# Branch C's triangular solve: forward by rows instead of columns, its blocks loaded by four transfers, and two short steps before it written otherwise

## The chip, the cores and the metric

The kernel runs on one core of a Trainium2 chip. The metric is device time in microseconds (us) for one call. TensorE (PE) does the matrix products, VectorE (DVE) and ScalarE (ACT) the elementwise work, GpSimd (POOL) some elementwise work and transfers, SyncE (SP) issues most of the transfers.

## The reference

One inference step of a decoder layer for a prompt group (1024 tokens) and a sample group (8 sequences of 8 new tokens). Four parallel token mixers, A to D, read one input projection of x. The change lies in branch C, a state recurrence over tokens with 4 heads of 64:

```
kk = kk / max(sqrt(sum(kk * kk)), 1e-12)
k_eff = k * (1.0 + (a - 1.0) * ka_s)
def step(S, inp):                       # -kk and kk * a are a_t and b_t
    sa = einsum('nhij,nhj->nhi', S, a_t)
    S = S * w_t[:, :, None, :] + sa[..., None] * b_t[:, :, None, :] + v_t[..., None] * k_t[:, :, None, :]
    return S, einsum('nhij,nhj->nhi', S, r_t)
y = (y - m) * rsqrt(var + RW_GN_EPS) * gn_g + gn_b
```

The other branches, the gates, the memory attention and the MLP follow; they are not changed.

## The kernel before

Branch C is done in chunks of 256 prompt tokens (numbers 0 to 3) and one chunk, number 4, for the 64 sample tokens, in the order 0, 4, 1, 2, 3. `branch_c` (L763 on) calls for each chunk `c_pre` (decays, k, r, v and the normalised kk), `c_blocks` (the strictly triangular products L of 128 x 128 per head and block), `c_solve` (the inverse of a unit triangular matrix in diagonal blocks of 32 x 32), `c_uw` (what the inverse is used for), `c_chain` or `c_sample` (the state itself) and `c_norm`. The next chunk's `c_pre`, `c_blocks` and `c_solve` stand in the text ahead of or beside the present chunk's chain.

`c_solve` writes the 32 x 32 diagonal blocks of L to DRAM (`Ld`, L1003), reads them back with one transfer that puts the same 32 blocks on four groups of 32 partitions (`Li`, L1004), and lets each partition carry eight rows of the inverse (`Ti`, which starts as the identity, `teye`, L1008). VectorE sets the diagonal of `Li` to one (L1009) and then makes one column t of `Ti` after the other: a product over all s up to t into `tpr` (L1015), and a sum over s (L1016), 31 columns, 62 instructions, for the sample as for the prompt. `Ti` then goes through DRAM (`Td`, L1018) into the block diagonal `TT` (L1021), from which `c_uw` starts (product u, L1036). `Li` and `Ti` have one buffer each.

`rsqrt` (L922) takes exp(-0.5 ln s) on ScalarE and betters it by one Newton step of five VectorE instructions (L927 to L931). It serves `c_pre` (kk) and `c_norm` at full width, and branch D at a few columns. In `c_pre`, L891 and L892 make k (1 + (a - 1) ka).

Between these steps `fill` puts units of other work into the text: the input projections of D, A and B (products mm, L118 and L130, whose weights come through `split_w`: transfer `wraw`, ScalarE's rounding `whi` L101, VectorE's rest `wlo` L107). Each engine's order is fixed when the program is built, by a planner that takes instructions by their place in the text and by durations of its own; every engine then runs its list in order, and a wait at its head holds all that is behind it. SP's list holds `wraw`, the raw rows of C (`raw<-hC`), `Ld`, `Li`, `teye`, `Td` and `TT` together.

Of the kernel before, what the change touches and what calls it, by code (L numbers as in the profile page):

```python
# [8 lines left out]
F32 = mybir.dt.float32  # L9
F32R = mybir.dt.float32r  # L10
I32 = mybir.dt.int32
AF = mybir.ActivationFunctionType
ALU = mybir.AluOpType
AX = mybir.AxisListType
# [8 lines left out]
C_BG, C_CONV, C_MU, C_W0, C_A0, C_KK, C_KA, C_RK, C_GNG, C_GNB, C_SB = 0, 32, 38, 45, 47, 49, 51, 53, 55, 57, 59  # L23
# [9 lines left out]
def sv(a, x):  # L33
    return a.rearrange("p (s x) -> p s x", x=x)
# [16 lines left out]
class Kern:  # L51
# [721 lines left out]
    def branch_c(self, cc):  # L773
        nc, I, O = self.nc, self.I, self.O
        vec = self.vec
        self.cc = cc
        cm = self.cm = cc.tile([128, 648], F32, name="cmask")
        self.lw = cc.tile([128, 256], F32, name="lw")
        self.smask = cc.tile([128, 320], F32, name="smask")
        self.omu = cc.tile([128, 7], F32, name="omu")  # L780
        for t, x in ((cm, "cmask"), (self.lw, "lora"), (self.smask, "smask")):
            nc.sync.dma_start(t, I[x])
        nc.vector.tensor_scalar(self.omu, vec[:, C_MU:C_MU + 7], -1.0, 1.0, op0=ALU.mult, op1=ALU.add)
        self.bones = cm[:, 0:128]

        self.S = [cc.tile([128, 2, 2, 64], F32, name=f"S{i}") for i in range(2)]
        for t in self.S:
            nc.vector.memset(t, 0.0)
        order = (0, 4, 1, 2, 3)
        TT = self.TT = cc.tile([128, 8, 128], F32, name="TT")  # L790
        nc.gpsimd.memset(TT, 0.0)
        d = self.c_pre(0)
        self.c_blocks(d)
        self.c_solve(d)
        nxt = self.c_pre(order[1])
        self.fill("first")
        for i, c in enumerate(order):
            if nxt:
                self.c_blocks(nxt)
            self.c_uw(d)  # L800
            if nxt:
                self.c_solve(nxt)
            if c < 4:
                self.c_chain(d)
            else:
                self.c_sample(d)
            after = self.c_pre(order[i + 2]) if i < 3 else None
            self.c_norm(d)
            d, nxt = nxt, after
        for hh in range(2):  # L810
            nc.gpsimd.dma_start(O["p_wkv"][HR[hh]], self.S[0][HR[hh], :, hh, :])

    def c_pre(self, c):

        nc, vec, cc = self.nc, self.vec, self.cc
        smp = c == 4
        n, x, o, w = (64, 8, 1025, 72) if smp else (256, 64, 256 * c, 257)
        ns = n // x
        V = lambda q, pr: vec[:, q + pr:q + pr + 1]
# [4 lines left out]
        def shifted(m, k, name, tag="t"):  # L824

            raw, xs = self.ct("raw"), self.cf(name, n, tag)
            nc.sync.dma_start(raw[:, :k, :w], self.hC[:, m:m + k, o:o + w])
            for i in range(k):
                mu, om = vec[:, C_MU + m + i:C_MU + m + i + 1], self.omu[:, m + i:m + i + 1]
                if smp:  # L830
                    cur, prev, out = sv(raw[:, i, 0:72], 9)[:, :, 1:9], sv(raw[:, i, 0:72], 9)[:, :, 0:8], sv(xs[:, i], 8)
                else:
                    cur, prev, out = raw[:, i, 1:n + 1], raw[:, i, 0:n], xs[:, i]
                nc.scalar.mul(out, prev, mu)
                nc.vector.scalar_tensor_tensor(out, cur, om, out, op0=ALU.mult, op1=ALU.add)
            return xs
# [6 lines left out]
        sg, a = self.cf("sg", n), self.cf("aa", n)  # L843
# [8 lines left out]
        k = shifted(2, 2, "xk")  # L852
# [35 lines left out]
        nc.vector.tensor_mul(bh, kk, a)  # L888
        nc.vector.tensor_mul(bh, bh, Pi)
        for pr in range(2):  # L890
            nc.vector.tensor_scalar(a[:, pr], a[:, pr], 1.0, V(C_KA, pr), op0=ALU.subtract, op1=ALU.mult)  # L891
        nc.vector.scalar_tensor_tensor(k, a, 1.0, k, op0=ALU.add, op1=ALU.mult)  # L892
        nc.vector.tensor_mul(kh, k, Pi)
        r = shifted(0, 2, "xr")
        nc.vector.tensor_mul(by(rt), by(r), Pp[:, :, 1:x + 1])
# [4 lines left out]
        for i in range(2):  # L900
            mu, om = vec[:, C_MU + 4 + i:C_MU + 5 + i], self.omu[:, 4 + i:5 + i]
            if smp:
                cur, prev, out = sv(raw[:, i, 0:72], 9)[:, :, 1:9], sv(raw[:, i, 0:72], 9)[:, :, 0:8], sv(v[:, i], 8)
            else:
                cur, prev, out = raw[:, i, 1:n + 1], raw[:, i, 0:n], v[:, i]
# [16 lines left out]
    def rsqrt(self, s, r, out):  # L922

        nc = self.nc
        nc.scalar.activation(r, s, AF.Ln)
        nc.scalar.activation(r, r, AF.Exp, scale=-0.5)
        nc.vector.tensor_mul(s, s, r)  # L927
        nc.vector.tensor_mul(out, out, r)
        nc.vector.tensor_mul(s, s, r)
        nc.vector.tensor_scalar(s, s, -0.5, 1.5, op0=ALU.mult, op1=ALU.add)  # L930
        nc.vector.tensor_mul(out, out, s)  # L931

    def c_blocks(self, d):

# [59 lines left out]
    def c_solve(self, d):  # L994

        nc, cc, c = self.nc, self.cc, d["c"]
        L = d["L"]
        Ld = self.dr.tile([4, 8, 32, 32], F32, name="Ld", tag=f"Ld{c}")
        Li = cc.tile([128, 32, 32], F32, name="Li", tag="Li")
        Ti = cc.tile([128, 8, 32], F32, name="Ti", tag="Ti")  # L1000
        tp = cc.tile([128, 8, 32], F32, name="tpr", tag="tpr")
        for q in range(4):
            nc.sync.dma_start(Ld[q].rearrange("(b h) s t -> s b h t", h=2), L[32 * q:32 * q + 32, :, :, 32 * q:32 * q + 32])  # L1003
        nc.sync.dma_start(Li.rearrange("p s t -> p (s t)"), Ld.rearrange("q i s t -> (q i) (s t)")[None].to_broadcast([4, 32, 1024]))  # L1004
        if c < 4:

            nc.gpsimd.tensor_mul(L, L, self.cm[:, None, None, 384:512].to_broadcast([128, 4, 2, 128]))
        nc.sync.dma_start(Ti, self.I["teye"])  # L1008
        nc.vector.memset(Li.rearrange("p a b -> p (a b)")[:, 0::33], 1.0)  # L1009
        tf = tp.rearrange("p a s -> p (a s)")  # L1010
        for t in range(1, 32):
            h = t // 4 + 1
            tv = tf[:, :h * (t + 1)].rearrange("p (a s) -> p a s", s=t + 1)

            nc.vector.tensor_mul(tv, Ti[:, 0:h, 0:t + 1], Li[:, 0:t + 1, t:t + 1].rearrange("p s o -> p o s").to_broadcast([128, h, t + 1]))  # L1015
            nc.vector.tensor_reduce(Ti[:, 0:h, t:t + 1], tv, axis=AX.X, op=ALU.add)  # L1016
        Td = self.dr.tile([4, 8, 8, 4, 32], F32, name="Td", tag=f"Td{c}")
        nc.sync.dma_start(Td.rearrange("q i l e t -> e (q i) l t"), Ti)  # L1018
        TT = self.TT
        for q in range(4):  # L1020
            nc.sync.dma_start(TT[32 * q:32 * q + 32, :, 32 * q:32 * q + 32], Td[q].rearrange("i l e t -> (l e) i t"))  # L1021
# [1353 lines left out]
```

## Time and profile before

| What | us |
|---|---|
| median of 3 runs | 2223.06 |
| lowest, highest run | 2218.23, 2223.72 |
| the profiled execution's own time | 2223.23 |
| its span | 2221.5 |
| PE busy in the span | 2140.5 (96%) |
| DVE busy | 1338.9 (60%) |
| ACT busy | 944.9 (43%) |
| POOL busy | 421.1 (19%) |

Busy is the time in which an engine had an instruction at work. A wait is the idle time of an engine ahead of an instruction, put down to what ended last before it. PEclk is the share of TensorE's full clock (2.4 GHz) that was granted; 0.50 is the lower level, 1.2 GHz. Branch C's chunks lie between 96 and 450 us of the span.

### The profile page before, as it was taken

The numbers are of one execution on the slowest core, as the hardware profiler recorded it, in microseconds if no ns is written. First come the engines' busy times: TensorE is split into PE (matmuls) and PEld (weight loads), VectorE is DVE, ScalarE is ACT, GpSimd is POOL, SyncE is SP. The second block draws the span as 40 slices with busy tenths as digits, with TensorE's granted clock in tenths as the row PEclk, the third lists the DMA queues.
The fourth block names the chain that finished last, engine by engine and source line by source line (L and its number), as shares of the span: only waits on it lengthen the run. The fifth ranks groups of instructions, "written<-read, shape, count | busy, mean of one in ns | idle before, by whom it ended". The sixth has DMA issues, their size and how long they took to land.

```text
span 2221.5 us, 36111 instructions
## 1 busy us (share of the span) xinstructions
PE 2140.5 (96%) x13674; PEld 1912.7 (86%) x13674; DVE 1338.9 (60%) x2682; ACT 944.9 (43%) x1838; POOL 421.1 (19%) x478
## 2 busy tenths in 40 slices
PE   8988999999999999999999999999999999999998
PEld 8977787888989988998899877779999999788886
DVE  3265778745666665343325583469877766665477
ACT  4343343234555556444323262326444444544341
POOL 0110111112310310013221230000654542100000
PEclk9999999999999999999999999999999999999999
DMA  6322333135543434555415145743686667976552
GB/s 196 98 75 59 100 106 93 41 121 178 152 135 116 151 103 159 172 169 164 128 48 194 57 159 188 251 157 124 239 278 234 237 243 252 322 250 203 166 199 90
DMA packets 184838, 356.11 MB, mean 160 GB/s; under 512 B 36104, under 2 KB 92568, under 8 KB 184664
## 3 DMA queue, kind: packets, MB, share of 16 engines
q1 hardware_dynamic: 174216, 318.24, 43.6%
q0 software_dynamic: 10448, 35.57, 4.7%
q8 instruction: 107, 1.75, 0.3%
q14 instruction: 67, 0.55, 0.1%
HBM read 250.01 MB, written 103.73 MB: 159 GB/s over the span
## 4 chain that ended last, share of the span: by engine, by line
PE 72%; DMA 10%; DVE 10%; ACT 3%; issue 3%; POOL 1%; SPq 1%; DVEq 0%; ACTq 0%; POOLq 0%
PE mm L118 20%; PE m L118 14%; PE dn L2037 13%; PE mm L130 8%; PE sc L130 3%; PE pp L118 3%; PE ds L2042 1%; DVE wlo L107 1%; DVE tpr L1015 1%; ACT whi L101 1%; DMA add<-gate 1%; PE gr L967 1%; DMA wraw<-in_w_gate 1%; DMA Li<-Ld 1%; DMA vp<-in_vpages,pt 1%
## 5 line engine op out<-in xcount | busy, mean ns | idle before, releaser
L118 PE MATMUL mm<-ah,whi 128*128 128x384 f32 (+1 forms) x1176 | 394.6, 336 | 10.3 <-ACT ah L279 5.1
L118 PE MATMUL mm<-al,whi 128*128 128x384 f32 (+1 forms) x1176 | 391.3, 333 | 1.4 <-DVE al L280 1.4
L118 PE MATMUL mm<-ah,wlo 128*128 128x384 f32 (+1 forms) x1176 | 390.7, 332 | 0.6 <-DVE wlo L107 0.6
L2037 PE MATMUL dn<-dop 128*128 128x512 f32 x1344 | 317.1, 391 | 1.9 <-ACT dop L1705 1.9
L2037 PEld LDWEIGHTS dn<-dop 128*128 128x128 f32 x1344 | 252.2, 188 | 56.7 <-ACT dop L1705 2.3
L107 DVE TENSOR_TENSOR wlo<-wraw,whi 128x1024 fp32r<-128x1024 f32 (+2 forms) x145 | 159.1, 1104 | 168.4 <-ACT whi L101 167.7
L118 PEld LDWEIGHTS mm<-ah,whi 128*128 128x128 f32 x1176 | 223.8, 190 | 19.9 <-ACT ah L279 5.4
L101 ACT CAST whi<-wraw 128x1024 fp32r<-128x1024 f32 (+1 forms) x130 | 132.9, 1028 | 227.6 <-PE mm L118 100.4
L118 PEld LDWEIGHTS mm<-al,whi 128*128 128x128 f32 x1176 | 223.2, 190 | 7.1 <-issue 3.3
L118 PEld LDWEIGHTS mm<-ah,wlo 128*128 128x128 f32 x1176 | 223.5, 190 | 4.2 <-issue 1.9
L1706 DVE TENSOR_TENSOR dop<-wraw,dop 128x512 fp32r<-128x512 f32 x224 | 149.1, 696 | 109.2 <-ACT dop L1705 109.0
L118 PE MATMUL m<-xht,wo 128*128 128x272 f32 x1024 | 199.3, 290 | 2.8 <-DVE u L1914 2.6
L1705 ACT CAST dop<-wraw 128x512 fp32r<-128x512 f32 x224 | 133.0, 620 | 153.9 <-PE dn L2037 85.8
L130 PE MATMUL mm<-wlo,ah 128*128 128x512 f32 (+1 forms) x488 | 169.2, 350 | 4.5 <-DVE wlo L107 4.4
L130 PE MATMUL mm<-whi,ah 128*128 128x512 f32 (+1 forms) x488 | 170.2, 351 | 0.6 <-ACT stA L302 0.5
L118 PEld LDWEIGHTS m<-xht,wo 128*128 128x128 f32 x1024 | 162.6, 188 | 3.7 <-ACT u L1734 2.8
L130 PE MATMUL mm<-whi,al 128*128 128x512 f32 (+1 forms) x448 | 156.2, 349 | 0.0
L118 PE MATMUL m<-xh,wo 128*128 128x272 f32 x768 | 150.8, 290 | 0.0
L118 PE MATMUL m<-xlt,wo 128*128 128x272 f32 x512 | 147.7, 289 | 1.4 <-DVE xlt L2184 1.4
L118 PEld LDWEIGHTS m<-xh,wo 128*128 128x128 f32 x768 | 122.4, 188 | 0.1
L118 PE MATMUL m<-xl,wo 128*128 128x272 f32 x384 | 110.7, 289 | 0.0
L130 PEld LDWEIGHTS mm<-wlo,ah 128*128 128x128 f32 x488 | 93.4, 192 | 18.6 <-DVE wlo L107 5.6
(514 smaller groups left out, 4211.2 us busy)
## 6 DMA issues: line engine op xcount, KB each, us to landing
wraw<-hs SPq DMA_DIRECT2D x112, 256.0 KB
wraw<-in_w_up SPq DMA_DIRECT2D x36, 512.0 KB
wraw<-in_w_gate SPq DMA_DIRECT2D x32, 512.0 KB
dw<-in_w_down SPq DMA_DIRECT2D x32, 512.0 KB
hs<-sh SPq DMA_DIRECT2D x64, 256.0 KB
wt<-dw SPq DMA_DIRECT2D x32, 512.0 KB
wraw<-wt SPq DMA_DIRECT2D x64, 256.0 KB
wraw<-in_w_down SPq DMA_DIRECT2D x48, 256.0 KB
```

The lines of the kernel that those rows point to most:

```text
L101: nc.scalar.copy(hi[:, c], raw[:, c])
L107: nc.vector.tensor_sub(lo[:, c], raw[:, c], hi[:, c].bitcast(F32))
L118: nc.tensor.matmul(ps[:, :n], a, b, start=first and i == 0, stop=last and i == len(steps) - 1, skip_group_check=not first)
L130: nc.tensor.matmul(ps[:, :n], a, b, start=i == 0, stop=i == len(steps) - 1)
L967: nc.tensor.matmul(g[hh][:nb, j, :nb], p[HR[hh], pr, cs], q[HR[hh], pr, cs], start=True, stop=True)
L1015: nc.vector.tensor_mul(tv, Ti[:, 0:h, 0:t + 1], Li[:, 0:t + 1, t:t + 1].rearrange("p s o -> p o s").to_broadcast([128, h, t + 1]))
L1705: nc.scalar.copy(o[:, 0], src)
L1706: nc.vector.tensor_sub(o[:, 1], src, o[:, 0].bitcast(F32))
L2037: nc.tensor.matmul(ps[j], hs[:, a, c], w[:, b], start=first and k == 0, stop=last and k == 2, skip_group_check=n >= 16 and steps[n][0] in ...
L2042: nc.tensor.matmul(sp, rows[p][:, smp[i]].rearrange("p a n -> p (a n)"), ops[n][1][:, b], start=i != 2 and p == 0 and b == 0, stop=p == 15 ...
```

## The change

- `c_solve` works by rows s: column s of `Ti` times row s of the blocks, to the right of the diagonal, into `tpr`, and then an addition of that to the rest of `Ti`: 31 rows, 62 instructions for a prompt chunk, over fewer elements. The diagonal is no longer used and no longer set.
- For the sample, whose blocks within each 32 x 32 are four of 8 x 8, one row of all four is done at once by a strided view: 7 rows, 14 instructions. The tiles get a row more for that view.
- `Li` is loaded by four transfers of 32 partitions, and `teye` stands ahead of `Ld` in the text.
- `rsqrt`'s Newton step has four VectorE instructions instead of five.
- (1 - ka) + a ka is made by two ScalarE instructions, and VectorE's product with k has no addition in it.

```diff
+        self.oka = cc.tile([128, 2], F32, name="oka")
+        nc.vector.tensor_scalar(self.oka, vec[:, C_KA:C_KA + 2], -1.0, 1.0, op0=ALU.mult, op1=ALU.add)
...
         for pr in range(2):
-            nc.vector.tensor_scalar(a[:, pr], a[:, pr], 1.0, V(C_KA, pr), op0=ALU.subtract, op1=ALU.mult)
-        nc.vector.scalar_tensor_tensor(k, a, 1.0, k, op0=ALU.add, op1=ALU.mult)
+            nc.scalar.activation(a[:, pr], a[:, pr], AF.Identity, scale=V(C_KA, pr), bias=self.oka[:, pr:pr + 1])
+        nc.vector.tensor_mul(k, a, k)
...
-        nc.vector.tensor_mul(s, s, r)
+        nc.vector.scalar_tensor_tensor(s, s, -0.5, r, op0=ALU.mult, op1=ALU.mult)
         nc.vector.tensor_mul(out, out, r)
         nc.vector.tensor_mul(s, s, r)
-        nc.vector.tensor_scalar(s, s, -0.5, 1.5, op0=ALU.mult, op1=ALU.add)
-        nc.vector.tensor_mul(out, out, s)
+        nc.vector.scalar_tensor_tensor(out, s, 1.5, out, op0=ALU.add, op1=ALU.mult)
...
-        Li = cc.tile([128, 32, 32], F32, name="Li", tag="Li")
-        Ti = cc.tile([128, 8, 32], F32, name="Ti", tag="Ti")
-        tp = cc.tile([128, 8, 32], F32, name="tpr", tag="tpr")
+        Li = cc.tile([128, 33, 32], F32, name="Li", tag="Li")
+        Ti = cc.tile([128, 9, 32], F32, name="Ti", tag="Ti")
+        tp = cc.tile([128, 80], F32, name="tpr", tag="tpr")
+        nc.sync.dma_start(Ti[:, 0:8], self.I["teye"])
...
-        nc.sync.dma_start(Li.rearrange("p s t -> p (s t)"), Ld.rearrange("q i s t -> (q i) (s t)")[None].to_broadcast([4, 32, 1024]))
+        for e in range(4):
+            nc.sync.dma_start(Li[32 * e:32 * e + 32, 0:32].rearrange("p s t -> p (s t)"), Ld.rearrange("q i s t -> (q i) (s t)"))
...
-        nc.sync.dma_start(Ti, self.I["teye"])
-        nc.vector.memset(Li.rearrange("p a b -> p (a b)")[:, 0::33], 1.0)
-        tf = tp.rearrange("p a s -> p (a s)")
-        for t in range(1, 32):
-            h = t // 4 + 1
-            tv = tf[:, :h * (t + 1)].rearrange("p (a s) -> p a s", s=t + 1)
-
-            nc.vector.tensor_mul(tv, Ti[:, 0:h, 0:t + 1], Li[:, 0:t + 1, t:t + 1].rearrange("p s o -> p o s").to_broadcast([128, h, t + 1]))
-            nc.vector.tensor_reduce(Ti[:, 0:h, t:t + 1], tv, axis=AX.X, op=ALU.add)
+            for s in range(31):
+                h, n = s // 4 + 1, 31 - s
+                tv = tp[:, :h * n].rearrange("p (a t) -> p a t", t=n)
+                nc.vector.tensor_mul(tv, Ti[:, 0:h, s:s + 1].to_broadcast([128, h, n]), Li[:, s:s + 1, s + 1:32].to_broadcast([128, h, n]))
+                nc.vector.tensor_add(Ti[:, 0:h, s + 1:32], Ti[:, 0:h, s + 1:32], tv)
+        else:
+
+            Tv = Ti.rearrange("p a t -> p (a t)").rearrange("p (b y) -> p b y", y=72)[:, :, 0:64].rearrange("p b (j t) -> p b j t", t=32)
+            Lv = Li.rearrange("p s t -> p (s t)").rearrange("p (b y) -> p b y", y=264)
+            for s in range(7):
+                n = 7 - s
+                tv = tp[:, :8 * n].rearrange("p (b j t) -> p b j t", j=2, t=n)
+                row = Lv[:, :, None, 32 * s + s + 1:32 * s + 8].to_broadcast([128, 4, 2, n])
+                nc.vector.tensor_mul(tv, Tv[:, :, :, s:s + 1].to_broadcast([128, 4, 2, n]), row)
+                nc.vector.tensor_add(Tv[:, :, :, s + 1:8], Tv[:, :, :, s + 1:8], tv)
```

## Rows read from the trace of the kernel before

**Rows 1.** Stretch: length, busy of PE, PEld, DVE, ACT, POOL; PEclk; DMA.

```profile
96.00:450.00 354.00, 323.85 (x2503) 272.53 (x2503) 245.40 (x720) 127.64 (x301) 48.74 (x81) 0.96 0.27 81
481.00:2221.50 1740.50, 1696.78 (x10416) 1527.31 (x10414) 1052.83 (x1852) 777.42 (x1459) 361.62 (x374) 0.99 0.54 179
```

**Rows 2.** Waits of PE from 96 to 450 us: total us, times, longest us.

```profile
PE u L1036 <- DMA TT<-Td: 9.8, 2, 9.4
PE gr L967 <- DVE bh L889: 4.1, 4, 1.8
PE mm L130 <- DVE wlo L107: 4.1, 1, 4.1
PE snp L1141 <- DVE ex L1120: 3.1, 1, 3.1
PE st L1094 <- DVE S L1090: 1.8, 4, 1.2
...
PE gr L967 <- DVE kh L893: 0.8, 1, 0.8
```

**Rows 3.** VectorE: its wait for Li in all, and rows of its timeline (start, us).

```profile
DVE Li L1009 <- DMA Li<-Ld: 17.7, 4, 8.8
...
140.09 0.09 DVE L1009 MEMSET Li<- 128x32 f32 x1 [4.01 <-DMA Li<-Ld]
...
142.31 2.49 DVE L107 TENSOR_TENSOR wlo<-wraw,whi 128x512 fp32r<-128x512 f32 x4
...
262.85 0.65 DVE L1120 TENSOR_TENSOR ex<-SAs,cmask 64x512 f32<-64x512 f32 x1 [4.68 <-issue]
262.87 0.09 DVE L1009 MEMSET Li<- 128x32 f32 x1
```

**Rows 4.** Chain of work that ended last (start, us): the first solve's transfers, the last one's Td.

```profile
129.74 10.26 DMA Li<-Ld
...
168.10 13.07 DMA Td<-Ti
...
182.53 1.94 DMA TT<-Td
...
431.51 4.85 DMA Td<-Ti
```

**Rows 5.** SP's timeline: the four TT issues (start, us for all).

```profile
181.19 1.79 SPq L1021 DMA_DIRECT2D TT<-Td  x4
```

**Rows 6.** One Li transfer running alone, by stretch; and a wraw transfer in the chain.

```profile
392.30:399.30 7.00, 7.00 (x64) 6.36 (x64) 1.38 (x2) 2.25 (x6) 0.32 (x1) 1.00 0.25 76
...
512.46 4.46 DMA wraw<-in_w_gate
```

**Rows 7.** Stretches 142.22:149.05, 184.61:190.01, 263.55:268.51, 340.19:347.02 summed; L130 alone in two.

```profile
sum 24.02, PE 23.10 PEld 19.39 DVE 15.44 ACT 6.81 POOL 2.06; mean PE 5.77 PEld 4.85 DVE 3.86 ACT 1.70 POOL 0.52
...
129.10:134.90 5.80, 5.80 (x52) 5.80 (x52) 1.00 0.25 56
143.10:147.90 4.80, 4.80 (x22) 4.71 (x22) 0.50 0.66 213
```

**Rows 8.** First solve, L1015 then L1016 busy; a smallest and a full-width product.

```profile
140.10:168.00 27.90, 10.39 (x31) 0.88 0.23 68
...
140.10:168.00 27.90, 7.80 (x31) 0.88 0.23 68
...
140.21 0.16 DVE L1015 TENSOR_TENSOR tpr<-Ti,Li 128x2 f32<-128x2 f32 x1
...
104.91 0.69 DVE L928 TENSOR_TENSOR kkv<-kkv,rs 128x512 f32<-128x512 f32 x1
```

**Rows 9.** VectorE's timeline: Newton, ka; ScalarE's Identity by form (mean ns).

```profile
106.32 0.41 DVE L930 TENSOR_SCALAR rn<-rn 128x512 f32<-128x512 f32 x1
...
110.54 0.60 DVE L891 TENSOR_SCALAR aa<-aa,vec 128x256 f32<-128x256 f32 x2
...
L1166 ACT ACTIVATE Y<-Y,vec 128x256 f32<-128x256 f32 x6 | 3.3, 594 | 5.5 <-DVE Y L931 5.5
```

More of the change, by code (lines that the diff above doesn't have):

```diff
@@ L1017, in c_solve @@
         Td = self.dr.tile([4, 8, 8, 4, 32], F32, name="Td", tag=f"Td{c}")
-        nc.sync.dma_start(Td.rearrange("q i l e t -> e (q i) l t"), Ti)
+        nc.sync.dma_start(Td.rearrange("q i l e t -> e (q i) l t"), Ti[:, 0:8])
         TT = self.TT
```

## The prediction

> **What bounds the kernel now.** I read the busy time by stretch first. After branch C, from 481 us to the end, PE is busy 1696.78 of 1740.5 us, so the rest of the kernel runs at PE's pace and a saving made earlier should reach the end whole. From 96 to 450 us, where C's chunks lie, PE is busy 323.85 of 354 us: 30 us idle, and VectorE is busy 245.40 us, the second resource [rows 1]. The work that PE has there is fixed by the text (so many fill units between the steps of C), so what can be won is that idle time and what PE loses at the lower clock level.
>
> The waits of PE in that stretch say whom it waits for [rows 2]: 9.4 us once for TT, the result of the first solve; 4.1 us once for a weight's wlo; 3.1 us once for ex of the sample; 1.2 us once for the state S; four waits for bh, 4.1 us together; 0.8 us for kh. VectorE's own timeline tells why three of these are long: VectorE stands at the head of a solve, at L1009, until Li has landed, 17.7 us in four waits, and what is queued behind cannot start. The wlo of 142.31 stands behind the wait of 4.01 us that ends at 140.09; ex starts at 262.85 after 4.68 us that the page gives to no one, and the next solve's L1009 is stamped 0.02 us later, so I take that to be the same wait (an inference) [rows 3].
>
> Then the chain: Li needs 10.26 us to land, Td of the first solve 13.07 us, Td of the last, with little beside it, 4.85 us [rows 4].
>
> Last the clock: in the four stretches at PEclk 0.50, PE is busy 23.10 us; the same products of L130 go 52 in 5.80 us at full clock and 22 in 4.80 us at half, a rate of 0.51, so 0.49 x 23.10 = 11.3 us of those are lost [rows 7]. Three of the four stretches begin during or just after the three longest waits named above.
>
> **The change part by part.**
>
> *Li in four transfers.* While one Li runs alone the DMA engines are busy for 0.25 of their time, and it takes about 10 us, where a wraw of the same 512 KB lands in 4.46 us [rows 4, 6]. So the present Li uses about a quarter of the engines, and four transfers with 32 partitions as their first dimension have no such copy dimension ahead. Estimate: three more issues at 1.79 / 4 = 0.45 us, then the landing of a 32-partition transfer, 1.94 us for TT (32 KB against 128 KB) up to 4.46 us for wraw: 3.3 to 5.8 us, I take 4.5, so 5.8 us sooner [rows 4, 5, 6]. Every VectorE wait for Li but the sample's 8.8 us is shorter than that, so the three PE waits behind them go: 4.1 + 3.1 + 1.2 = 8.4 us. If Li lands only 2 us sooner, about half stays: 4.
>
> The Trainium skill, "DMA: Bandwidth & Descriptors", "Rules for kernel authors", speaks against it: two transfers to disjoint partition halves serialize on the same engines, and one of 128 partitions is to be used instead. By that rule Li would land no sooner and the 8.4 would be nothing; what that makes of the time is the first rival.
>
> *The solve.* Before: 10.39 + 7.80 = 18.2 us in 62 instructions. A smallest product takes 0.16 us and a full-width one 0.69, so an instruction costs 0.158 us and 1.04 ns an element [rows 8]. After, for the prompt: 62 instructions over 1560 elements twice: 62 x 0.158 + 3120 x 0.00104 = 13.0 us, 5.2 less; at worst each costs what it did (0.29 us on average) and nothing is won. For the sample: 14 instructions over 224 elements twice, 2.7 us, 15.5 less. That is 36 us off VectorE in all, most of it beside PE's work, so it counts at nothing except through the wait for TT. There the times add: Li 5.8 sooner, solve 5.2 shorter, and Td between 4.85 and 13.07 us; the 13.07 us had the sample's Li issued just ahead of it, on the same quarter of the engines if my reading holds, so I take 7, 6.1 sooner [rows 4]. Together 17.1 us. PE comes to u sooner too, by the 4.1 us wait and by its lost work in the first half-clock stretch (0.49 x about 6 = 2.9 us): the wait of 9.4 plus 7.0 is 16.4. So TT is there just in time; I leave 1 us and count 8.4. With Td at 13.07 again, 5.4 us stay and it is 4.0.
>
> *The clock.* With these waits gone three of four half-clock stretches lose their cause. I take 0.85 x 11.3 = 9.6 us; bounds 4 (a shorter wait still drops the clock) and 11.3 [rows 7].
>
> *Newton.* One instruction of 0.41 us fewer; the others keep their width and about their time [rows 9]. It lies on PE's path at the waits for bh alone: four times 0.41, at most 1.6; I take 1.5, bounds 0 and 1.6 [rows 2, 9]. In c_norm and branch D it lies beside other work.
>
> *(1 - ka) + a ka on ScalarE.* It takes 0.60 us off VectorE per prompt chunk and puts two ScalarE instructions of 0.59 us there, with a hand-over each way [rows 9]. ScalarE waits for VectorE's bh product, which still reads a, and behind it on ScalarE stand the roundings whi and the next rows of C. VectorE has the second bh product and r's work meanwhile, so k comes between 0.5 us sooner and 1.2 us later; the only wait for kh is 0.8 us [rows 2]. I take 0.5 later four times: -2.0, bounds +2 and -4.8.
>
> *SP's list.* The four issues hold SP 1.35 us longer per chunk, ahead of raw rows and weights; `teye`, now ahead of `Ld` in the text, still has to wait until the Td before has read Ti. I take -1.0 in all, bounds 0 and -5 (five chunks by about 1 us) [rows 5]. The removed setting of the diagonal, 0.09 us, and the new `oka` count at nothing; POOL's list is passed by nothing.
>
> Sum: 8.4 + 8.4 + 9.6 + 1.5 - 2.0 - 1.0 = 24.9 us. The profiled execution took 2223.23 us, the median of the runs is 2223.06, so the same sum serves for both: 2223.2 - 24.9 = 2198.3. All upper bounds together give 8.4 + 9.4 + 11.3 + 1.6 + 2 = 32.7 us, 2190; all lower ones 4 + 4 + 4 - 4.8 - 5 = 2.2 us, 2221. What is late next: the waits for bh, rn and kh of c_pre, which stay as short as they are, and products waiting for S.
>
> **The rivals.**
>
> *Li lands no sooner.* The waits of 4.1 and 3.1 us and their clock stretches stay. TT is then sooner by the solve's 5.2 us alone, and perhaps 2 us of clock with it, and the other terms take 1.5: 5.2 + 2 - 1.5 = 5.7 us, 2217.5. For it: four transfers still share one set of engines. Against it: the share of 0.25, and a wraw of the same size in half the time [rows 6].
>
> *The planner sets u and the solves earlier.* It knows that a solve is shorter, and may put PE's u and VectorE's first solve step earlier by more than the transfers have gained; then VectorE stands for Li and PE for TT again, for shorter times. Half of the three large terms comes back: 24.9 - 13.2 = 11.7 us, 2211.5. For it: the present order already put PE at u 9.4 us too soon [rows 2].
>
> *The gain does not reach the end.* A stage after C that waits for something else takes it up to 5 us from the start: 2218. Against it: PE's 97.5% there [rows 1].
>
> *Slower: ScalarE held by the ka step.* ScalarE runs its list in order, and the two new instructions wait there for VectorE's product of kk and a, after the whole Newton chain. If the planner puts them early, the whi of the next weight waits behind them, wlo with it, and PE has no weights: each of the four prompt chunks then costs a wait like that of 4.1 us, 1.5 us more of it as the chain is longer than Li's rest, and a half-clock stretch of 2.9 us, 34 us in all against the 24.9: +9, 2232. It decides from the point at which ScalarE stands longer than the weights in hand last. Against it: ScalarE is busy 127.64 of 354 us there [rows 1].
>
> **How the numbers follow.** Forecast 0.66; Li no sooner 0.08; planner 0.14; gain lost on the way 0.06; slower 0.06. The predicted time is the likeliest one's, 2198. 0.3% of the time, about what a measurement of this kernel can tell from no change, is 6.7 us: faster means under 2216.4. The forecast and the planner's case lie there, and a little of the first rival: 0.82. Within: 0.12. Slower: 0.06. The range runs from 2187 (the upper bounds, and 3 us that a VectorE freer by 36 us may give at the remaining waits) to 2218, which leaves out the slower case, half of the lost gain and a few hundredths on both sides.
>
> **What would show it.** Right: Li landing 3 to 6 us after its first issue with a DMA share well above 0.25; solves of 62 instructions in about 13 us busy and 14 in about 3; no PE wait for wlo or ex of over 1 us, and for TT at most 1 or 2; at most two half-clock stretches from 96 to 430 us; PE's idle time in C's chunks from 30 to some 12 us; the time from 481 us on as long as now. Wrong: Li at 10 us again; a new PE wait for whi or wlo at the ka step; a wait for TT of 5 us; or later stages longer than before.

## The result and the profile after

The changed kernel takes 2193.73 us, the median of four runs from 2193.3 to 2194.85. The kernel before took 2220.64 us beside it (four runs, 2210.98 to 2223.72). The ratio is 0.9884, with a 95% interval of 0.9859 to 0.9908: 26.9 us less, faster. In the last experiment the same kernel gave 0.99, some 21 us, so the gain is 21 to 27 us. The profiled execution took 2193.3 us, against 2223.23 for the one of before, which is in the upper part of its runs. The forecast was 2198, with a range from 2187 to 2218.

The page of the kernel after, its span and the busy time of each engine:

```profile
span 2191.5 us, 36073 instructions
...
PE 2133.3 (97%) x13674; PEld 1905.9 (87%) x13674; DVE 1308.3 (60%) x2607; ACT 948.9 (43%) x1848; POOL 420.8 (19%) x478
```

VectorE is 30.6 us less busy, while the span is 30.0 us shorter; the two figures are alike by chance: taking the work off VectorE alone gives nothing (R alone, below). The stretches of the kernel after (columns as in [rows 1]):

```profile
96.00:450.00 354.00, 344.00 (x2716) 289.32 (x2714) 222.83 (x678) 134.82 (x314) 52.43 (x88) 0.99 0.28 84
...
453.50:2191.50 1738.00, 1696.46 (x10416) 1525.80 (x10414) 1056.31 (x1851) 777.52 (x1459) 361.11 (x374) 0.99 0.54 179
```

In the same 354 us PE is busy 344.00 us where it was 323.85, and does 2716 products where it did 2503 [rows 1]. From the end of C's last product to the end of the span it takes about what it took: 1737.6 us against 1740.1, with the same 10416 products in the second row of each kernel. So 27.5 of the 30.0 us by which these two executions differ come from branch C, which ends at 453.9 us instead of 481.4.

Within C two things changed, both counted from the trace's PE rows from 96 us to C's end: PE's idle time went from 30.2 to 10.0 us, and its busy time at the lower clock level (PEclk 0.50) from 23.1 to 6.8 us. At the rate of [rows 7] the latter is 0.49 x 16.3 = 8.0 us. 20.2 + 8.0 = 28.2 us, against the 27.5 by which C ends sooner.

PE's waits in the kernel after, 96 to 450 us (total us, times, longest us):

```profile
PE hs L921 <- ACT rn L882: 4.1, 3, 2.1
PE gr L968 <- DVE tpr L1015: 1.0, 1, 1.0
PE st L1087 <- DVE Y L1105: 0.9, 4, 0.3
PE gr L968 <- DVE bh L891: 0.7, 2, 0.4
PE u L1046 <- DMA TT<-Td: 0.7, 1, 0.7
...
PE st L1104 <- DVE S L1100: 0.3, 1, 0.3
```

Against [rows 2]: the 9.8 us for TT are 0.7, the 4.1 for wlo and the 3.1 for ex are gone, bh has 0.7 where it had 4.1, and S is down from 1.8 to 0.3. One wait is new in size: rn, ScalarE's square of kk in `c_pre`, 4.1 us in all. Before had:

```profile
PE hs L919 <- ACT rn L880: 1.2, 3, 0.6
```

The two stretches of the kernel after in which the granted clock is 0.50, and the one in which the last Li lands (columns as in [rows 1], DMA share and GB/s last):

```profile
151.30:154.71 3.41, 3.41 (x20) 3.07 (x20) 2.93 (x15) 0.37 (x2) 0.00 (x0) 0.50 0.13 19
257.11:260.52 3.41, 3.41 (x13) 3.41 (x12) 3.17 (x12) 2.52 (x4) 1.12 (x2) 0.50 0.10 41
...
361.60:366.00 4.40, 4.40 (x38) 4.13 (x38) 0.14 (x1) 2.02 (x6) 2.36 (x1) 1.00 0.42 123
```

Before had four half-clock stretches with 23.10 us of busy PE [rows 7]; two are left, with 6.82. In the third row 123 GB/s over 4.40 us are 0.54 MB, and Li has 0.52 MB, so the four transfers had landed within 4.4 us of the first issue, at a DMA share of 0.42. Before, the first Li took 10.26 us, and the last, running alone, had a share of 0.25 [rows 4, 6]. The trace also marks when each DMA engine has ended its part of a transfer. By these marks Li is there 4.0 us after its first issue in three of the prompt's four chunks, and after 8.9 us in the third, where a weight's and raw rows' transfers run beside it (DMA share 0.91 from 291.6 to 301 us). VectorE waits for Li nowhere in the kernel after.

The first solve of the kernel after, by stretch: L1015 alone (length, busy and count; L1016 has the same figures), then L1025 of the sample:

```profile
138.20:156.20 18.00, 6.42 (x31) 0.91 0.22 73
...
160.00:175.00 15.00, 1.31 (x7) 1.00 0.49 130
```

SP's timeline around that solve (start, us for all):

```profile
126.57 1.72 SPq L1007 DMA_DIRECT2D Li<-Ld  x4
...
156.20 0.63 SPq L1028 DMA_DIRECT2D Td<-Ti  x1
156.88 4.51 SPq L1007 DMA_DIRECT2D Li<-Ld  x2
162.90 1.80 SPq L1031 DMA_DIRECT2D TT<-Td  x4
```

Twice 6.42 is 12.8 us for the prompt's 62 instructions, where before had 18.2 [rows 8], and twice 1.31 is 2.6 for the sample's 14. TT is issued at 162.90 instead of 181.19 [rows 5].

### The profile page after: what moved, and what is told of

It is laid out like the page before. It is cut to its first block, busy times and chain, and to the rows that moved or that the text cites. A ratio compares the mean times of both kernels' runs of the same rounds, so it can differ in the third digit from the quotient of the medians.

```text
span 2191.5 us, 36073 instructions
## 1 busy us (share of the span) xinstructions
PE 2133.3 (97%) x13674; PEld 1905.9 (87%) x13674; DVE 1308.3 (60%) x2607; ACT 948.9 (43%) x1848; POOL 420.8 (19%) x478
## 4 chain that ended last, share of the span: by engine, by line
PE 78%; DMA 7%; DVE 7%; ACT 4%; issue 3%; POOL 1%; SPq 1%; DVEq 0%; ACTq 0%; POOLq 0%
PE mm L118 21%; PE m L118 15%; PE dn L2047 13%; PE mm L130 9%; PE sc L130 3%; PE pp L118 2%; PE ds L2052 1%; PE gr L968 1%; ACT whi L101 1%; PE wtp L504 1%; DVE wlo L107 1%; PE hs L921 1%; DMA add<-gate 1%; DMA wraw<-in_w_gate 1%; POOL mix L1327 1%
## 5 line engine op out<-in xcount | busy, mean ns | idle before, releaser
L130 PE MATMUL mm<-whi,ah 128*128 128x512 f32 (+1 forms) x488 | 168.9, 348 | 0.5 <-ACT stD L643 0.5
L130 PE MATMUL mm<-wlo,ah 128*128 128x512 f32 (+1 forms) x488 | 167.4, 346 | 0.3 <-DVE wlo L107 0.3
L130 PE MATMUL mm<-whi,al 128*128 128x512 f32 (+1 forms) x448 | 155.3, 347 | 0.0
L130 PEld LDWEIGHTS mm<-whi,ah 128*128 128x128 f32 x488 | 92.3, 189 | 13.9 <-issue 1.2
```

The costliest lines, as they stand in the source:

```text
L130: nc.tensor.matmul(ps[:, :n], a, b, start=i == 0, stop=i == len(steps) - 1)
```

## The experiments

Three parts are told apart: L, the four Li transfers; R, the solve by rows, with the sample's seven, the unset diagonal and `teye` ahead of `Ld`; S, the two short steps (Newton and ka). Kernels of one session share their runs of before, and each ratio is to these, with its 95% interval. Every kernel computes the whole. The planner lays all engines' orders anew for each text, which no experiment here could hold still.

### L alone

```
-        nc.sync.dma_start(Li..., Ld...[None].to_broadcast([4, 32, 1024]))
+        for e in range(4):
+            nc.sync.dma_start(Li[32 * e:32 * e + 32]..., Ld.rearrange("q i s t -> (q i) (s t)"))
```

> The kernel before with one edit: Li by four transfers of 32 partitions. Theory A (most of the gain is transfer time, through VectorE's wait for Li and PE's wait for TT, with the clock stretches behind them): Li lands 4 to 6 us after its first issue, the PE waits for wlo and ex are under 1 us, the wait for TT shrinks from 9.4 to about 5 us, and the kernel is 16 to 20 us faster than before. Theory B (most of the gain is VectorE's saved work): 5 us faster at most. Theory C (the four transfers serialize like one): Li lands after 10 us and there is no gain.

Measured: 2221.26 us, ratio 1.0016 [0.9995, 1.0038], twelve runs. Nothing is won, which is Theory B's time, but not for its reason, as the next experiment shows. SP's timeline at the first solve (start, us for all):

```profile
163.42 0.63 SPq L1019 DMA_DIRECT2D Td<-Ti  x1
...
168.39 2.12 SPq L1022 DMA_DIRECT2D TT<-Td  x4
```

The transfers do what they should: TT is issued 12.8 us sooner than in [rows 5], 5.0 us after Td, where before Td took 13.07 [rows 4], and PE's waits for TT sum to 1.0 us. But PE has other waits in the same stretch, 96 to 450 us:

```profile
PE gr L967 <- DVE rt L895: 7.3, 2, 5.5
PE mm L118 <- DVE yB L613: 4.4, 1, 4.4
```

VectorE's timeline ahead of the longest one (start, us):

```profile
280.71 0.68 DVE L893 TENSOR_TENSOR kh<-xk,sg 128x512 f32<-128x512 f32 x1
281.31 0.58 DVE L1016 TENSOR_TENSOR tpr<-Ti,Li 128x256 f32<-128x256 f32 x1
281.81 0.47 DVE L835 SCALAR_TENSOR_TENSOR xr<-raw,omu,xr 128x256 f32<-128x256 f32 x1
282.21 0.41 DVE L1017 TENSOR_REDUCE Ti<-tpr 128x8 f32<-128x256 f32 x1
...
283.32 0.68 DVE L895 TENSOR_TENSOR rt<-xr,Pp 128x512 f32<-128x512 f32 x1
```

The solve's columns lie one by one between the steps of `c_pre`, and rt, which PE wants from 278.6 on, comes after the last column. From 268 to 283.3 us VectorE is busy 15.13 of 15.30 us, and 8.4 of them go to 20 instructions of the solve. yB stands behind the last solve in the same way. With the data there in time, VectorE's own work is what ends last.

### R alone

```
-            nc.vector.tensor_mul(tv, Ti[:, 0:h, 0:t + 1], Li[:, 0:t + 1, t:t + 1]...)
-            nc.vector.tensor_reduce(Ti[:, 0:h, t:t + 1], tv, axis=AX.X, op=ALU.add)
+                nc.vector.tensor_mul(tv, Ti[:, 0:h, s:s + 1]..., Li[:, s:s + 1, s + 1:32]...)
+                nc.vector.tensor_add(Ti[:, 0:h, s + 1:32], Ti[:, 0:h, s + 1:32], tv)
```

The sample has its seven rows too; Li comes by one transfer, Newton and ka are as before.

> The kernel before with the solve by rows (and the sample's 14 instructions) alone: one Li transfer, Newton and ka as before. The four transfers alone gave no gain, and their trace showed PE waiting 5.45 us for rt where the next solve lay on VectorE among c_pre's steps. Theory J (joint: PE waits for the later of the transfers and VectorE's queue, so either part alone moves the wait to the other): 8 us faster at most, with PE waits behind Li and for TT. Theory S (the prediction's separate terms): the solve's term alone, about 5 us faster. Theory V (VectorE's work is all that counts): 15 us or more faster.

Measured: 2218.86 us, ratio 1.0005 [0.9982, 1.0027], twelve runs. Nothing is won either, with VectorE 28.9 us less busy (1310.0 us), so VectorE's work is not all that counts. PE's waits (96 to 450 us):

```profile
PE u L1044 <- DMA TT<-Td: 8.5, 2, 8.1
PE st L1091 <- DVE SA L1086: 6.0, 2, 5.4
```

The chain that ended last, the first solve's transfers (start, us):

```profile
128.25 8.88 DMA Li<-Ld
...
157.99 13.11 DMA Td<-Ti
```

SP's timeline shows what was issued ahead of Td, the sample's Li (start, us):

```profile
157.41 0.54 SPq L1005 DMA_DIRECT2D Li<-Ld  x1
157.99 0.55 SPq L1026 DMA_DIRECT2D Td<-Ti  x1
```

The solve ends about 10 us sooner than in [rows 4], Td still takes 13.11 us, and PE waits 8.1 us for TT, about as long as before. The wait of 5.4 us for SA stands behind a transfer too: VectorE's SA of 328.39 us comes right after the first step of a solve, which has waited 8.74 us for Li. VectorE's waits for transfers (96 to 450 us):

```profile
DVE tpr L1023 <- DMA Ti<-in_teye: 17.7, 1, 17.7
DVE tpr L1013 <- DMA Li<-Ld: 15.4, 4, 8.7
```

The first is the sample's identity, whose transfer may not start until Td has read `Ti`. Before, VectorE had 17.7 us for Li [rows 3] and this:

```profile
DVE tpr L1015 <- DMA Ti<-in_teye: 8.4, 1, 8.4
```

So VectorE stands for transfers 33.1 us where it stood 26.1: part of the time that its shorter solve frees goes there. Here the transfers end last.

### S alone

```
-            nc.vector.tensor_scalar(a[:, pr], a[:, pr], 1.0, V(C_KA, pr), ...)
-        nc.vector.scalar_tensor_tensor(k, a, 1.0, k, op0=ALU.add, op1=ALU.mult)
+            nc.scalar.activation(a[:, pr], a[:, pr], AF.Identity, scale=V(C_KA, pr), bias=self.oka[:, pr:pr + 1])
+        nc.vector.tensor_mul(k, a, k)
...
-        nc.vector.tensor_scalar(s, s, -0.5, 1.5, op0=ALU.mult, op1=ALU.add)
-        nc.vector.tensor_mul(out, out, s)
+        nc.vector.scalar_tensor_tensor(out, s, 1.5, out, op0=ALU.add, op1=ALU.mult)
```

> The kernel before with Newton's step and the ka step alone changed. It takes about 1 us off VectorE per prompt chunk and c_norm. Theory J: within 5 us of the kernel before, the waits for Li and TT as before. Theory S: within 2 us. If it is 8 us or more faster, these two steps are a cause of their own.

Measured: 2216.59 us, ratio 1.0001 [0.998, 1.0021], twelve runs. Waits for TT (7.2 us in all) and bh (4.8 us) stand about as in [rows 2].

### All but L

The changed kernel with Li by one transfer again.

```
-        for e in range(4):
-            nc.sync.dma_start(Li[32 * e:32 * e + 32, 0:32]..., Ld...)
+        nc.sync.dma_start(Li[:, 0:32]..., Ld...[None].to_broadcast([4, 32, 1024]))
```

> The changed kernel with one edit undone: Li again by one transfer with the four copies as its first dimension. Theory A: Li takes about 10 us, VectorE stands for it in front of each solve, PE waits of 2 to 4 us for wlo or ex come back, and only 6 to 12 us of the change's 27 us are left. Theory B: at least 20 us of the gain stay. Theory C: nothing is lost.

Measured: 2208.48 us, ratio 0.9958 [0.994, 0.9976], ten runs: 13 to 16 us of the gain are lost (against 0.99 and 0.9884), as Theory A has it. The waits that come back are not those that it names, for wlo or ex, but for TT, for bh (3.9 us) and for SA (3.8 us). PE's longest, 96 to 450 us:

```profile
PE u L1045 <- DMA TT<-Td: 7.0, 1, 7.0
```

The chain that ended last, around it (start, us):

```profile
158.00 4.69 DMA Td<-Ti
164.05 8.74 DMA TT<-Td
```

On SP's list the sample's Li was issued just ahead of TT (start, us for all):

```profile
158.68 2.18 SPq L1006 DMA_DIRECT2D Li<-Ld  x1
162.71 1.79 SPq L1030 DMA_DIRECT2D TT<-Td  x4
```

TT is issued as early as in the changed kernel (162.90), and Td took 4.69 us. What is long is TT's own transfer: 8.74 us, where it took 1.94 before [rows 4]. The marks of the DMA engines tell why. Li has four of them, from 171.3 to 172.0 us, besides one soon after its issue. The TT transfer issued at 164.05 has sixteen: twelve come 2.0 to 2.6 us after its issue, four 8.1 to 8.7 us after it, right behind Li's. So part of what the four transfers give is not that Li comes sooner but that what follows on the queue is not held up by it.

### All but S, and all but R

The changed kernel with Newton and ka as before (the diff of S undone):

> The changed kernel without Newton's and the ka step: Li in four transfers and the solve by rows. Theory J: both halves of the cause are here, so 18 to 25 us faster than before; PE waits in C's chunks about as short as with the whole change. Theory S: 23 to 26 us faster. If the two steps carry much of the gain, 10 us faster or less.

Measured, L and R without S: 2196.7 us, ratio 0.99 [0.9877, 0.9923], six runs. PE's waits, 96 to 450 us:

```profile
PE hs L919 <- ACT rn L880: 3.0, 3, 1.9
...
PE u L1045 <- DMA TT<-Td: 0.3, 1, 0.3
```

There is none for rt or yB, and VectorE waits neither for Li nor for the identity.

The kernel before with the diffs of L and of S, and its solve by columns:

> Li in four transfers with Newton's and the ka step, the solve still by columns with 62 instructions for every chunk. Theory J: VectorE is still held by the long solve at c_pre's steps, so 10 us faster at most, with PE waits for rt or bh of several us. Theory S: 17 us or more faster.

Measured, L and S without R: 2216.36 us, ratio 0.999 [0.9973, 1.0006], twelve runs. PE's waits, 96 to 450 us:

```profile
PE mm L118 <- DVE yB L613: 3.4, 1, 3.4
PE hs L921 <- ACT rn L882: 2.6, 2, 2.1
PE gr L968 <- DVE rt L897: 2.6, 2, 1.8
PE u L1038 <- DMA TT<-Td: 2.0, 2, 1.1
```

yB and rt again, as with L alone: VectorE.

All of it in one table. Idle and half-clock time of PE are counted from 96 us to C's end, from the profiled execution of each. Those executions lie at different places among their runs (that of R alone is the slowest of its twelve), so the ratio says what an edit is worth, and the columns behind it where PE stood.

| kernel | ratio | PE idle | PE at half clock | C ends at | VectorE waits for Li and identity |
|---|---|---|---|---|---|
| before | 1 | 30.2 | 23.1 | 481.4 | 26.1 |
| L | 1.0016 | 28.6 | 13.8 | 473.4 | 2.0 |
| R | 1.0005 | 27.8 | 38.1 | 485.6 | 33.1 |
| S | 1.0001 | 26.5 | 17.8 | 476.8 | 24.3 |
| L, S | 0.999 | 18.5 | 26.8 | 472.1 | 1.4 |
| R, S | 0.9958 | 23.3 | 18.7 | 469.1 | 28.9 |
| L, R | 0.99 | 11.6 | 20.5 | 458.1 | 0 |
| L, R, S | 0.9884; again 0.99 | 10.0; 10.2 | 6.8; 17.1 | 453.9; 458.2 | 0; 0 |

L alone and R alone gain nothing (at most 4 us, by the lower end of the two intervals), and together 1% (22 us), at intervals that do not meet. S alone gains nothing that can be told either; R and S together gain 0.4% (9 us). PE at a step of C waits for the later of two things, a transfer and VectorE's list; each part makes one of them shorter, and the other then ends last. That the other takes over is shown by the waits above: without L VectorE waits 24 to 33 us for transfers, whatever else is changed; with L but without R PE waits for VectorE at rt and yB, 11.7 us in all with L alone and 6.0 us with L and S; with both, neither is left. How much of it is VectorE's load and how much the order that the planner makes of it was not separated, nor what `teye`'s new place gives within R.

The clock alone does not make the 22 us. The time of one kernel moves with the granted clock: of the 59 runs of before beside these experiments, the nine at a mean clock of 0.990 or more took 2207.6 to 2217.0 us, the five under 0.985 took 2222.3 to 2227.4. L and R together had 0.988 to 0.993 and took 2192.3 to 2202.1. Their mean clock is 0.9905, that of before in the same session 0.9873. By the slope of these runs of before, 2.1 us for 0.001, about 7 of the 22 us go with the clock, an estimate.

### The sample's 14 instructions, and the ka step

The changed kernel with the 31 rows (62 instructions) for the sample too:

```
-            if c < 4: ... else: (seven rows, four blocks at once)
+            for s in range(31): (as for the prompt)
```

> The changed kernel with the sample's solve done as the prompt's: 31 rows, 62 instructions, instead of 7 rows, 14 instructions. It puts some 10 us of work back on VectorE. Theory A: that work lies beside PE's, and the time changes by less than 3 us. Theory B: the time grows by 8 to 10 us.

Measured: 2191.14 us, ratio 0.9883 [0.9859, 0.9908], five runs, the same as the changed kernel. VectorE is busy 230.93 us from 96 to 450 us instead of 222.83. Those 8 us lie beside PE's work and cost nothing that can be told; the interval spans 11 us.

The changed kernel with the ka step on VectorE as before:

```
-            nc.scalar.activation(a[:, pr], a[:, pr], AF.Identity, scale=V(C_KA, pr), bias=self.oka[:, pr:pr + 1])
-        nc.vector.tensor_mul(k, a, k)
+            nc.vector.tensor_scalar(a[:, pr], a[:, pr], 1.0, V(C_KA, pr), op0=ALU.subtract, op1=ALU.mult)
+        nc.vector.scalar_tensor_tensor(k, a, 1.0, k, op0=ALU.add, op1=ALU.mult)
```

> The changed kernel with (1 - ka) + a ka as before, on VectorE. The prediction put the move to ScalarE at a loss of 2 us (bounds: a gain of 2, a loss of 4.8), so this should be 2 us faster than the changed kernel, with no PE wait for kh. If the move is a gain, it is slower by up to 2 us.

Measured: 2195.27 us, ratio 0.9907 [0.9882, 0.9933], six runs. No difference from the changed kernel can be told. In the changed kernel the two ScalarE instructions wait little (lines by form: total us, mean ns, idle before):

```profile
L893 ACT ACTIVATE aa<-aa,oka,vec 128x256 f32<-128x256 f32 x8 | 4.4, 594 | 1.2 <-DVE bh L890 1.1
```

### Li in two transfers

To see what makes a Li slow, the changed kernel with two transfers of 64 partitions, each with two copies ahead:

```
-        for e in range(4): (as above)
+        for e in range(2):
+            nc.sync.dma_start(Li[64 * e:64 * e + 64, 0:32]..., Ld...[None].to_broadcast([2, 32, 1024]))
```

> The changed kernel with Li by two transfers of 64 partitions, each with the two copies as its first dimension. If the first dimension of a transfer sets how many DMA engines it uses (one transfer with four copies showed 0.25 of them busy), each of these uses an eighth, both perhaps the same eighth, and the two need 10 to 20 us to land: VectorE stands for Li longer than in the kernel before, and the kernel is no faster than that one, perhaps 5 to 20 us slower. If it is the number of transfers in flight that helps, Li lands in 5 to 6 us and most of the gain stays.

Measured: 2246.29 us, ratio 1.0132 [1.0102, 1.0163], four runs: slower than one transfer (0.9958), and slower than before. The chain that ended last, the second transfer of its first Li (start, us; the first was issued at 126.71):

```profile
127.41 14.62 DMA Li<-Ld
```

A stretch in which the last Li runs with little beside it (columns as in [rows 1], DMA share and GB/s last):

```profile
400.00:408.00 8.00, 8.00 (x73) 7.34 (x74) 1.38 (x2) 2.61 (x8) 1.13 (x1) 1.00 0.13 41
```

The DMA share is 0.13, half of the 0.25 of [rows 6]: a quarter of sixteen engines are four, 0.13 of them two. The marks say the same: besides the early one, a Li transfer with four copies ahead has four and one with two copies two; TT has sixteen. The second transfer does not add two engines of its own. It takes 14.62 us. PE's waits, 96 to 450 us:

```profile
PE u L1046 <- DMA TT<-Td: 13.7, 1, 13.7
PE gr L968 <- DVE bh L891: 9.0, 3, 7.4
PE st L1104 <- DVE S L1100: 7.8, 3, 6.9
```

So it is not the number of transfers that helped but that their first dimension is the 32 partitions.

### Td in four transfers, and the changed kernel again

Td of the changed kernel has four groups as the first dimension of its DRAM side. The same cure:

```
-        nc.sync.dma_start(Td.rearrange("q i l e t -> e (q i) l t"), Ti[:, 0:8])
+        for e in range(4):
+            nc.sync.dma_start(Td[:, :, :, e].rearrange("q i l t -> (q i) l t"), Ti[32 * e:32 * e + 32, 0:8])
```

> The changed kernel with Td too written by four transfers of 32 partitions instead of one whose DRAM side has the four groups as its first dimension. Td should land in 2 to 3 us instead of 4.7 to 6.7. PE waits for TT 0.7 us in all in the changed kernel, so the time changes by less than 3 us, unless the planner makes more of it.

Measured: 2187.07 us, ratio 0.9858 [0.9837, 0.9879], four runs. SP's timeline at the first solve (start, us for all):

```profile
156.11 2.76 SPq L1029 DMA_DIRECT2D Td<-Ti  x4
...
160.29 1.80 SPq L1032 DMA_DIRECT2D TT<-Td  x4
```

The landing of all Td and TT issues, from the view of the tile Td:

```profile
DMA to landing us min/median/max: 1.9/2.0/3.6
```

From Td's first issue to TT's it takes 4.2 us, 6.7 in the changed kernel. Beside it ran the changed kernel itself, with no edit:

> The changed kernel as it is, beside the two variants of it on the same chip, for the small terms: the sample's 14 instructions and the ka step on ScalarE. The sum of the prediction has the first at nothing and the second at a loss of 2 us; 23 to 28 us faster than the kernel before.

and Td in four with two buffers for Ti:

```
-        Ti = cc.tile([128, 9, 32], F32, name="Ti", tag="Ti")
+        Ti = cc.tile([128, 9, 32], F32, name="Ti", tag="Ti", bufs=2)
```

> The changed kernel with Td by four transfers and two buffers for Ti, so that the sample's identity need not wait for the first Td. VectorE's wait for it and the sample's late solve go; PE has 10 us of idle time left in C's chunks, little of it behind these, so 0 to 4 us faster than the changed kernel.

Measured, the changed kernel: 2198.49 us, ratio 0.99 [0.9881, 0.992], five runs from 2194.55 to 2203.65. Two buffers: 2191.7 us, 0.988 [0.9859, 0.99], five runs. So Td in four is the fastest kernel of this study, 11 us below the changed kernel on the same chip, but not shown to be so for the reason it was made; less than 3 us were expected. The traces compared are the second fastest of its four runs and the slowest of the changed kernel's five. PE's idle time in C is 9.4 us against 10.2. Most of the rest lies in the clock (3.4 us of busy PE at half clock against 17.1, 0.49 x 13.7 = 6.7 us) and after C (1735.9 us against 1743.7). Two buffers, with the same Td, has 13.7 us at half clock and lies between the two; whether the second buffer does anything can't be told.

## Why the prediction was right, and where it was not

**Li lands in 4.5 us**: right, 4.0 to 4.4, but for the third prompt chunk (8.9), where VectorE came later than Li in any case. The three PE waits behind VectorE's wait (4.1, 3.1 and 1.2 us) went, or all but 0.3 us. The rival "Li lands no sooner" is answered by the runs: four transfers are there in less than half the time of one. The Trainium skill's rule against two transfers to disjoint partition halves ("DMA: Bandwidth & Descriptors", "Rules for kernel authors") says of them that both spread over all sixteen engines and so serialize. The single Li did not spread so, so the rule does not describe the change that it was held against. The Trainium skill has the rule that decided here in the same section: an outermost dimension of c < 16, such as a broadcast of c copies, confines a transfer to at most c engines. The shares 0.25 with four copies and 0.13 with two, and the four and two marks, agree with it.

**The solve**: 12.8 us for 13.0, the sample 2.6 for 2.7. **TT**: a wait of 0.7 us is left where 1 was, so 9.1 us for 8.4. TT's issue is 18.3 us sooner where 17.1 were worked out, but not by the terms as I gave them. Td gave 6.4 (6.1 expected). The solve's first step starts at 138.3 where it started at 140.2, 1.9 sooner where Li's landing was to give 5.8: VectorE has the sample's `c_pre` and a wlo ahead of it. The solve itself, with what is laid between its steps, takes 18.0 us where it took 27.9 [rows 8], 9.9 where 5.2 were expected. Two errors of opposite sign, so that this term came out by luck. That Td was held up by the sample's Li was right: it takes 13.1 us behind one (before, R alone) and 5.0 with the four (L alone).

**The clock**: 8.0 us for 9.6 in this execution, two stretches as forecast. In the profiled execution of the same kernel in the last experiment it was 17.1 us of half-clock time, which leaves 0.49 x 6.0 = 2.9 us, with the same waits to 0.3 us. This term moves by several us from run to run, and the forecast gave it one value; that it came near 9.6 is luck of the execution.

**Newton, ka, SP**: 1.5, -2.0 and -1.0. The waits for bh fell by 3.4 us where 1.5 was counted, but little of that is Newton's: with L and R and no S they sum to 1.1 us. The ka step made no wait at ScalarE worth the name (1.1 us in all, at 594 ns an instruction, the rows' figure). S is worth nothing that can be told alone, with L (0.9973 to 1.0006) or with L and R, and some 10 us with R (1.0005 to 0.9958), which no single term of mine says. rn, named as a wait that stays short, grew to 4.1 us, and is the longest now.

**PE's idle time in C**: 30 to "some 12", measured 10.0. **The rest**: "as long as now", 2.5 us shorter in this execution and 3.6 longer in the other (1743.7), so it is no part of the gain that can be claimed.

**The other rivals**: the planner did not set u or the solves ahead of their data (TT 0.7 us, no wait of VectorE for Li), nothing after C took the gain, and ScalarE was not held: PE's one wait for whi is 0.7 us long.

**The step that was wrong** is the one that the number does not show: that 36 us off VectorE "counts at nothing except through the wait for TT", and with it that Li's 8.4 us, TT's 8.4 and the clock's 9.6 add up, each for itself. By that sum L alone should have given at least its 8.4 us, and gave none; with L and S in place R still gives 20 to 23 us (0.999 to 0.99 and 0.9884), where the wait for TT that it could shorten is 2.0 us. VectorE's list at yB and rt is second in line behind the waits that L removes, and the views I read show only the first. The other way round, R alone ends at the transfers: there VectorE waits 33.1 us for Li and the identity, of which the prediction read only the part for Li. The prompt's solve is where VectorE's work matters: the sample's, 8 us of it, can be put back at no cost that can be told. The time came out because all parts were made together.

## What to carry to other kernels

Where PE waits now for a transfer and now for VectorE in the same steps, cut both before judging either: here neither alone was worth anything that could be told, and the two together 22 us. A wait that goes away says what ended last and not what ends next, so price a saving by the gap to the second in line, which the trace of an edit that removes only the first will show. Before a transfer is split or left whole, look at the DMA share while it runs alone: here a share of 0.25 meant that four of sixteen engines carried it.

## What the runs showed of the hardware that was not expected

Two broadcast transfers with two copies each are slower than one with four: 14.62 us against 10.26 [rows 4], at a DMA share of 0.13 against 0.25. In the prompt's four chunks the second transfer takes 13.6 to 16.6 us, against 8.7 to 11.5 for the single one in all kernels that have it. Both run on the same two engines: with both ahead of it, fourteen of the sixteen marks of a TT transfer come 2.0 to 2.2 us after its issue (177.41 us), and only two late, after 7.3 and 7.7.

A small transfer issued behind a broadcast Li is held up, on the engines alone that carry Li: TT took 8.74 us there, with four of its sixteen marks late, and about 2 us elsewhere.

A product that reads a column of Li costs more an element than one over a plain row: in the timeline of L alone 0.58 us for 128 x 256, beside 0.68 for a plain product of 128 x 512. At the same size, 128 x 60, the solve's product took 0.27 us by columns (before) and 0.22 by rows (after). The two differ in the views of both operands, and the column was not tried by itself. The instructions of the solve by rows took 0.21 us on average (12.8 / 62), what the estimate from plain products gave.
